# The sink logit as a column of the score tile, in a step of windowed attention

## The chip, the cores and the metric

The kernel runs on one core of one Trainium2 chip. The metric is the device time of one execution in microseconds (us). The engines are TensorE (PE; its weight loads are shown apart as PEld), VectorE (DVE), ScalarE (ACT), GpSimd (POOL) and SyncE (SP), which issues most of the DMAs.

## The reference

One inference step of a two-layer network over 128 context and 1024 latent tokens. Each layer has a token mixer of three groups (windowed softmax attention, gated linear attention, a recurrent unit) and an MLP. The change concerns the softmax of the attention group: 8 heads of 64 in 2 key groups, blocks of 128 queries, and per head one learned sink logit that takes part in the maximum and in the denominator and has no value row.

```python
def softmax_with_sink(scores, sink):
    m = sink
    for s in scores:
        m = jnp.maximum(m, jnp.max(s, axis=-1, keepdims=True))
    es = [jnp.exp(s - m) for s in scores]
    denom = jnp.exp(sink - m)
    for e in es:
        denom = denom + jnp.sum(e, axis=-1, keepdims=True)
    inv = 1.0 / denom
    return [e * inv for e in es]
```

A latent block sees its own, the previous and the next block of keys (masked to a distance of 128) and all 128 context keys in one softmax; a context block sees context keys alone.

## The kernel before

All arithmetic is fp32, with every matmul operand split into a high and a low part, so that a product is three matmuls (`dense`, lines 151 to 159), or two where one side is not split. `Net.layer` runs mixer, attention, output projection and MLP of one layer after the other.

`attention` works through 18 steps in each layer, one for a query block i and a key group g with four heads each, and a 19th turn that only finishes the last. In turn n, `scores` makes the scores of step n: per head two matmuls of up to 512 columns (L1061) into a PSUM bank, and one DVE instruction (L1063) that scales them, adds the mask, writes them to a tile P in SBUF and leaves the maximum, started from the sink logit, in a column of m. `soft` turns two heads at a time into probabilities: it negates m (L1072), adds the sink (L1073), takes the exponential of that (L1074, ACT), takes the exponential of P with bias m and the row sum (L1076, ACT), adds the two sums (L1077), inverts (L1078), and multiplies P by the inverse on POOL (L1080). The first half of `soft` is called inside `scores` after the second head, the second half later, between the pieces of `values`, which in the same turn works on the step before: it transposes P block by block on TensorE (L1089), splits it into ph (ACT, L1092) and pl (DVE, L1093) and multiplies with the values (L1098). A tile P has eight buffers, so two steps of four.

Between these pieces `attention` calls `fill` (in `layer`), which puts other TensorE work there: half an output tile of the output projection at a time (`out_half`, L1204 to L1211: two passes of two inputs with three matmuls each, 384 columns), and pieces of the modulation matrix (L249). Every fourth turn has one more half tile. The weights of the output projection are loaded and split by `load_w` (L117 to L119); in most of these stretches the subtraction L119 of 128x1024 runs on POOL.

TensorE's instructions stand in the order of the code. On the other engines a scheduler sets the order when the program is built, by its own estimate of when operands are there; every engine works through its list in order, so an instruction that waits holds all behind it. PSUM has five banks of `pg` for scores, transposes and values, two of `pd` for the output projection.

Of the kernel before, what the change touches and what calls it, by code (L numbers as in the profile page):

```python
# [48 lines left out]
class Net:  # L49
# [951 lines left out]
    def attention(self, l, fill):  # L1001
# [7 lines left out]
        nc.sync.dma_start(sink, I["attn_sink"][l:l + 1].to_broadcast([128, 8]))  # L1009
        for i in range(2, 4):  # L1010
            self.pre_q(0, i)
        def load_v():
# [34 lines left out]
        def scores(i, g, Q):  # L1047
            c0 = 128 * (i % 3)
            kpos, npos, vb, mk = geom(i)
            W = 128 * npos  # L1050
            m = ap.tile([128, 4], F32, tag="m", name="m", bufs=3)
            dn = ap.tile([128, 4], F32, tag="dn", name="dn", bufs=3)
            es = ap.tile([128, 4], F32, tag="es", name="es", bufs=3)
            Ps = []
            sc = (Ps, m, dn, es, W)
            for j in range(4):
# [3 lines left out]
                for ki, K in enumerate((KH[g], KL[g])):  # L1060
                    nc.tensor.matmul(ps[:, :W], q, K[:, kpos:kpos + npos].rearrange("p b c -> p (b c)"), start=ki == 0, stop=ki == 1)  # L1061
                P = ap.tile([128, 512], F32, tag="P", name="P", bufs=8)
                nc.vector.tensor_tensor_reduce(P[:, :W], ps[:, :W], mask[:, mk], scale=0.125, scalar=sink[:, h:h + 1],  # L1063
                                               op0=ALU.add, op1=ALU.max, accum_out=m[:, j:j + 1])
                Ps.append(P)
                if j == 1:
                    soft(g, 0, *sc)
            return sc

        def soft(g, part, Ps, m, dn, es, W):  # L1070
            js = slice(2 * part, 2 * part + 2)
            nc.vector.tensor_scalar(m[:, js], m[:, js], -1.0, None, ALU.mult)  # L1072
            nc.vector.tensor_tensor(es[:, js], sink[:, 4 * g + 2 * part:4 * g + 2 * part + 2], m[:, js], ALU.add)  # L1073
            nc.scalar.activation(es[:, js], es[:, js], AF.Exp)  # L1074
            for j in range(2 * part, 2 * part + 2):
                nc.scalar.activation(Ps[j][:, :W], Ps[j][:, :W], AF.Exp, bias=m[:, j:j + 1], accum_out=dn[:, j:j + 1])  # L1076
            nc.vector.tensor_tensor(dn[:, js], dn[:, js], es[:, js], ALU.add)  # L1077
            nc.vector.reciprocal(dn[:, js], dn[:, js])  # L1078
            for j in range(2 * part, 2 * part + 2):
                nc.gpsimd.tensor_scalar(Ps[j][:, :W], Ps[j][:, :W], dn[:, j:j + 1], 1.0, ALU.mult, ALU.mult)  # L1080

# [42 lines left out]
        for n in range(19):  # L1124
            if n < 18:
# [14 lines left out]
                sc = scores(i, g, Q)  # L1140
                if n == 1:
                    k1()
            if n:
                fill(n, 1)
                for k, _ in enumerate(values(*pend)):
                    if n < 18 and k == 1:
                        soft(g, 1, *sc)
                    fill(n, 2 + k)
            else:
                soft(g, 1, *sc)  # L1150
                load_v()
                k1 = self.load_k(l, 1, ap)
            pend = (i, g, sc[0])
# [373 lines left out]
```

## Time and profile before

| | us |
|---|---|
| runs (3), median (lowest to highest) | 2958.36 (2957.66 to 2959.3) |
| span of the profiled execution | 2958.0 |
| PE busy | 2765.4 |
| DVE busy | 1591.8 |
| ACT busy | 1069.0 |
| POOL busy | 796.3 |

The profile is of one execution; its span goes from the first to the last instruction and holds nearly all of its time. Matmuls overlap in the pipeline, so PE's busy time counts more than the time in which it delivers columns. Attention is the stretch from about 446 to 638 us in layer 0 and from 1892 to 2083 us in layer 1.

### The profile page before, as it was taken

Reading aid. Unit: us, or ns where it says so; the run is one execution under the profiler, and the core shown is the slowest. Engines: PE = TensorE matmul, PEld = TensorE weight load, DVE = VectorE, ACT = ScalarE, POOL = GpSimd, SP = SyncE. Lnnn points to the kernel's source line nnn. Section 1 sums busy time; section 2 is a strip of 40 time slices with the busy share of each in tenths; the row PEclk is TensorE's granted clock in tenths of the full one; section 3 lists DMA queues with packets and bytes.
Section 4 is the critical chain, followed back from the end, with each engine's and each line's share of the span. In section 5 each row is a group of like instructions: output and inputs, shape, how many; then the busy total and the mean of one; then the engine's idle time right before and its main releaser. Section 6 shows DMA issues by size and latency. Waiting matters only on the chain.

```text
span 2958.0 us, 41898 instructions
## 1 busy us (share of the span) xinstructions
PE 2765.4 (93%) x16067; PEld 2628.4 (89%) x16067; DVE 1591.8 (54%) x3032; ACT 1069.0 (36%) x2029; POOL 796.3 (27%) x807
## 2 busy tenths in 40 slices
PE   5897988989999999999987989899899999999998
PEld 3786987789999999999987879777899999999998
DVE  7668578896332332233478577888932332233235
ACT  4424446764122112211354326477622112211223
POOL 5323445652011001100133334466411001100112
PEclk7998999999999999999999999999999999999999
DMA  7535347411321111111333643662211111111113
GB/s 258 133 109 148 117 136 244 140 61 53 98 94 43 43 43 43 43 43 43 98 109 90 174 132 103 200 197 75 72 43 43 43 43 43 43 43 40 40 44 129
DMA packets 279304, 273.66 MB, mean 93 GB/s; under 512 B 30032, under 2 KB 259008, under 8 KB 279104
## 3 DMA queue, kind: packets, MB, share of 16 engines
q1 hardware_dynamic: 278888, 270.92, 29.7%
q8 instruction: 127, 2.08, 0.3%
q14 instruction: 73, 0.60, 0.1%
q10 hardware_dynamic: 216, 0.06, 0.0%
HBM read 227.02 MB, written 43.91 MB: 92 GB/s over the span
## 4 chain that ended last, share of the span: by engine, by line
PE 71%; DVE 16%; issue 4%; ACT 4%; POOL 3%; DMA 2%; SPq 0%; DVEq 0%; POOLq 0%; ACTq 0%
PE pg L155 18%; PE pg L156 18%; PE pg L157 18%; PE pd L155 2%; PE pd L156 2%; PE pd L157 2%; DVE B L672 2%; PE pg L1098 2%; PE pg L1061 1%; PE pe L249 1%; PE pd L1204 1%; DVE P L1063 1%; PE pd L1205 1%; PE pd L1206 1%; DVE wl L119 1%
## 5 line engine op out<-in xcount | busy, mean ns | idle before, releaser
L118 ACT CAST wh<-wr 128x1024 fp32r<-128x1024 f32 x228 | 238.9, 1048 | 931.1 <-PE pg L156 826.0
L156 PE MATMUL pg<-hl,wh 128*128 128x384 f32 x1584 | 538.3, 340 | 2.7 <-DVE hl L345 1.5
L155 PE MATMUL pg<-hh,wh 128*128 128x384 f32 x1584 | 538.8, 340 | 1.8 <-ACT hh L344 1.8
L157 PE MATMUL pg<-hh,wl 128*128 128x384 f32 x1584 | 537.4, 339 | 0.0
L1247 POOL TENSOR_TENSOR te<-te 128x384 f32<-128x384 f32 x192 | 166.7, 868 | 1331.5 <-ACT uh L1246 1331.3
L155 PE MATMUL pg<-uh,wh 128*128 128x384 f32 x1536 | 515.0, 335 | 0.6 <-ACT wh L118 0.6
L157 PE MATMUL pg<-uh,wl 128*128 128x384 f32 x1536 | 514.0, 335 | 1.7 <-DVE wl L119 1.7
L156 PE MATMUL pg<-ul,wh 128*128 128x384 f32 x1536 | 513.9, 335 | 0.0
L1269 DVE SCALAR_TENSOR_TENSOR x<-pg,mod,x 128x384 f32<-128x384 f32 (+2 forms) x512 | 254.1, 515 | 396.5 <-PE pg L157 396.3
L1248 DVE TENSOR_TENSOR ul<-te,uh 128x384 fp32r<-128x384 f32 x192 | 107.1, 558 | 452.6 <-POOL te L1247 452.6
L119 DVE TENSOR_TENSOR wl<-wr,wh 128x1024 fp32r<-128x1024 f32 x196 | 244.9, 1249 | 191.3 <-ACT wh L118 191.2
L155 PE MATMUL pd<-hh,wh 128*128 128x384 f32 x816 | 295.3, 362 | 24.8 <-DVE te L480 9.5
L155 PEld LDWEIGHTS pg<-hh,wh 128*128 128x128 f32 x1584 | 299.6, 189 | 5.4 <-issue 3.4
L156 PEld LDWEIGHTS pg<-hl,wh 128*128 128x128 f32 x1584 | 299.5, 189 | 5.1 <-DVE hl L351 2.5
L157 PEld LDWEIGHTS pg<-hh,wl 128*128 128x128 f32 x1584 | 299.3, 189 | 0.0
L155 PEld LDWEIGHTS pg<-uh,wh 128*128 128x128 f32 x1536 | 288.8, 188 | 4.3 <-issue 1.7
L157 PEld LDWEIGHTS pg<-uh,wl 128*128 128x128 f32 x1536 | 288.9, 188 | 2.1 <-DVE wl L119 2.0
L156 PEld LDWEIGHTS pg<-ul,wh 128*128 128x128 f32 x1536 | 288.8, 188 | 0.0
L156 PE MATMUL pd<-hl,wh 128*128 128x384 f32 x816 | 284.6, 349 | 3.4 <-DVE hl L385 3.4
L157 PE MATMUL pd<-hh,wl 128*128 128x384 f32 x816 | 284.0, 348 | 0.0
L1245 ACT ACTIVATE te<-pg 128x384 f32<-128x384 f32 x192 | 94.0, 489 | 358.9 <-PE pg L157 358.9
L155 PEld LDWEIGHTS pd<-hh,wh 128*128 128x128 f32 x816 | 161.2, 198 | 34.5 <-DVE te L480 10.8
(275 smaller groups left out, 4457.2 us busy)
## 6 DMA issues: line engine op xcount, KB each, us to landing
wr<-in_w_mlp_dram SPq DMA_DIRECT2D x144, 512.0 KB
wm<-in_w_mod_dram SPq DMA_DIRECT2D x96, 512.0 KB
wr<-in_w_out_dram SPq DMA_DIRECT2D x48, 512.0 KB
wr<-in_w_in_dram SPq DMA_DIRECT2D x36, 512.0 KB
xd<-x SPq DMA_DIRECT2D x48, 192.0 KB
x<-xd SPq DMA_DIRECT2D x48, 192.0 KB
raw<-mixd SPq DMA_DIRECT2D x40, 192.0 KB
B<-gkd SPq DMA_DIRECT2D x16, 288.0 KB
```

Source lines behind the costliest of these rows:

```text
L118: nc.scalar.copy(hi[:, :m], raw[:, :m])
L119: lo_eng.tensor_tensor(lo[:, :m], raw[:, :m], f32(hi[:, :m]), ALU.subtract)
L155: mm(out, wh[i], xs[i][0], start=i == 0, stop=False)
L156: mm(out, wh[i], xs[i][1], start=False, stop=False)
L157: mm(out, wl[i], xs[i][0], start=False, stop=i == n - 1)
L249: nc.tensor.matmul(p[32 * g:32 * g + 32, :], self.cs[:, kt, :], ws[g // 2][:, 512 * (g % 2):512 * (g % 2) + 512], start=kt == 0, stop=kt = ...
L672: nc.vector.scalar_tensor_tensor(out, Sc[r, c], dec[r, c:c + 1], dc[r, c], ALU.mult, ALU.add)
L1098: nc.tensor.matmul(po, VS[g][:, vb[b]], K, start=b == 0 and ki == 0, stop=b == npos - 1 and ki == 1)
L1245: nc.scalar.activation(r, p[:, :TB], AF.Relu)
L1247: nc.gpsimd.tensor_tensor(r, r, r, ALU.mult)
L1248: nc.vector.tensor_tensor(blk(ul, tb), r, f32(blk(uh, tb)), ALU.subtract)
L1269: nc.vector.scalar_tensor_tensor(xa, p[:, a:b], self.M[l]["g2"][:, dt, s:s + 1], xa, ALU.mult, ALU.add)
```

## The change

The sink is negated once per layer (nsink). Scores are written negated (scale -0.125), with a running minimum that starts from the negated sink, so that m holds the negated maximum without a further instruction. P becomes a tile of 4 rows of 513 elements for all four heads, held in two fixed buffers by the parity of the step; scores are written right-aligned, up to column 511, and column 512 holds the negated sink, copied by POOL (L1058 of the changed kernel). One exponential with scale -1 covers the scores and the sink column, and its row sum is the whole denominator. The lines L1072, L1073, L1074 and L1077 are gone. The line numbers of the changed kernel are 4 to 5 higher at the scores and 1 higher at the exponential; L1078, L1080 and those behind stay.

```diff
@@ -1007,8 +1007,12 @@
         nc.sync.dma_start(mask, C["c_amask"])
         sink = ap.tile([128, 8], F32, name="sink")
         nc.sync.dma_start(sink, I["attn_sink"][l:l + 1].to_broadcast([128, 8]))
+        nsink = ap.tile([128, 8], F32, name="nsink")
+        nc.vector.tensor_scalar(nsink, sink, -1.0, None, ALU.mult)
+        PT = [ap.tile([128, 4, 513], F32, name=f"P{k}") for k in range(2)]
         for i in range(2, 4):
             self.pre_q(0, i)
+
         def load_v():
             vraw = self.kp.tile([128, 10, 128], F32, tag="raw", name="vraw")
             nc.sync.dma_start(vraw[:, 0:9], self.vd.rearrange("j p c -> p j c"))
@@ -1044,40 +1048,36 @@
                 return 8, 3, [9, 7, 8], slice(0, 384)
             return KPOS[n - 1], 4, ([n, 9, n + 1, n + 2] if n % 2 == 0 else [n, n + 1, 9, n + 2]), slice(128, 640)
 
-        def scores(i, g, Q):
+        def scores(n, i, g, Q):
             c0 = 128 * (i % 3)
             kpos, npos, vb, mk = geom(i)
             W = 128 * npos
+            P = PT[n % 2]
             m = ap.tile([128, 4], F32, tag="m", name="m", bufs=3)
             dn = ap.tile([128, 4], F32, tag="dn", name="dn", bufs=3)
-            es = ap.tile([128, 4], F32, tag="es", name="es", bufs=3)
-            Ps = []
-            sc = (Ps, m, dn, es, W)
+            nc.gpsimd.tensor_copy(P[:, :, 512], nsink[:, 4 * g:4 * g + 4])
+            Ps = [P[:, j, 512 - W:512] for j in range(4)]
+            sc = (P, Ps, m, dn, W)
             for j in range(4):
                 h = 4 * g + j
                 ps = self.pg()
                 q = Q[h][:, c0:c0 + 128]
                 for ki, K in enumerate((KH[g], KL[g])):
                     nc.tensor.matmul(ps[:, :W], q, K[:, kpos:kpos + npos].rearrange("p b c -> p (b c)"), start=ki == 0, stop=ki == 1)
-                P = ap.tile([128, 512], F32, tag="P", name="P", bufs=8)
-                nc.vector.tensor_tensor_reduce(P[:, :W], ps[:, :W], mask[:, mk], scale=0.125, scalar=sink[:, h:h + 1],
-                                               op0=ALU.add, op1=ALU.max, accum_out=m[:, j:j + 1])
-                Ps.append(P)
+                nc.vector.tensor_tensor_reduce(Ps[j], ps[:, :W], mask[:, mk], scale=-0.125, scalar=nsink[:, h:h + 1],
+                                               op0=ALU.add, op1=ALU.min, accum_out=m[:, j:j + 1])
                 if j == 1:
-                    soft(g, 0, *sc)
+                    soft(0, *sc)
             return sc
 
-        def soft(g, part, Ps, m, dn, es, W):
+        def soft(part, P, Ps, m, dn, W):
             js = slice(2 * part, 2 * part + 2)
-            nc.vector.tensor_scalar(m[:, js], m[:, js], -1.0, None, ALU.mult)
-            nc.vector.tensor_tensor(es[:, js], sink[:, 4 * g + 2 * part:4 * g + 2 * part + 2], m[:, js], ALU.add)
-            nc.scalar.activation(es[:, js], es[:, js], AF.Exp)
             for j in range(2 * part, 2 * part + 2):
-                nc.scalar.activation(Ps[j][:, :W], Ps[j][:, :W], AF.Exp, bias=m[:, j:j + 1], accum_out=dn[:, j:j + 1])
-            nc.vector.tensor_tensor(dn[:, js], dn[:, js], es[:, js], ALU.add)
+                e = P[:, j, 512 - W:513]
+                nc.scalar.activation(e, e, AF.Exp, bias=m[:, j:j + 1], scale=-1.0, accum_out=dn[:, j:j + 1])
             nc.vector.reciprocal(dn[:, js], dn[:, js])
             for j in range(2 * part, 2 * part + 2):
-                nc.gpsimd.tensor_scalar(Ps[j][:, :W], Ps[j][:, :W], dn[:, j:j + 1], 1.0, ALU.mult, ALU.mult)
+                nc.gpsimd.tensor_scalar(Ps[j], Ps[j], dn[:, j:j + 1], 1.0, ALU.mult, ALU.mult)
 
         def values(i, g, Ps):
             kpos, npos, vb, mk = geom(i)
@@ -1137,20 +1137,20 @@
                     Q = {}
                     for j in range(4):
                         load_q(n // 6, j)
-                sc = scores(i, g, Q)
+                sc = scores(n, i, g, Q)
                 if n == 1:
                     k1()
             if n:
                 fill(n, 1)
                 for k, _ in enumerate(values(*pend)):
                     if n < 18 and k == 1:
-                        soft(g, 1, *sc)
+                        soft(1, *sc)
                     fill(n, 2 + k)
             else:
-                soft(g, 1, *sc)
+                soft(1, *sc)
                 load_v()
                 k1 = self.load_k(l, 1, ap)
-            pend = (i, g, sc[0])
+            pend = (i, g, sc[1])
         self.close(ag)
 
     def out_open(self, l):
```

The scheduler's order around it, in step 8 of layer 0 (query block 3, second key group). On DVE before, from the second score on (P and m carry numbers of their instances, es and dn too; pd is the output projection's bank):

```order
L1063 ISA P_4971,m_4960<-pg_4968,amask_4062,sink_4064 128x512 [waits PE_49,Pool_49]
L1063 ISA m_4960 128x1
L1063 ISA P_4985,m_4960<-pg_4982,amask_4062,sink_4064 128x512 [waits PE_49,Pool_49]
L1063 ISA m_4960 128x1
L1072 TENSOR_SCALAR m_4960<-m_4960 128x2 [waits DVE_49]
L1063 ISA P_4990,m_4960<-pg_4987,amask_4062,sink_4064 128x512 [waits PE_49,Pool_49]
L1063 ISA m_4960 128x1
L1073 TENSOR_TENSOR es_4962<-sink_4064,m_4960 128x2 [waits DVE_49]
L1211 SCALAR_TENSOR_TENSOR x5_3774<-pd_4911,mod0_1_2864,x5_3774 128x384 [waits DMAHW7_49,PE_49]
L1072 TENSOR_SCALAR m_4960<-m_4960 128x2 [waits DVE_49]
L1073 TENSOR_TENSOR es_4962<-sink_4064,m_4960 128x2 [waits DVE_49]
L1077 TENSOR_TENSOR dn_4961<-dn_4961,es_4962 128x2 [waits Activation_49]
```

On DVE now, the same place:

```order
L1067 ISA P1_4069,m_4880<-pg_4887,amask_4062,nsink_4066 128x512 [waits PE_49,Pool_49]
L1067 ISA m_4880 128x1
L1067 ISA P1_4069,m_4880<-pg_4896,amask_4062,nsink_4066 128x512 [waits PE_49,Pool_49]
L1067 ISA m_4880 128x1
L1067 ISA P1_4069,m_4880<-pg_4900,amask_4062,nsink_4066 128x512 [waits PE_49,Pool_49]
L1067 ISA m_4880 128x1
L1211 SCALAR_TENSOR_TENSOR x5_3774<-pd_4831,mod0_1_2864,x5_3774 128x384 [waits PE_49]
L1078 RECIPROCAL dn_4881<-dn_4881 128x2 [waits Activation_49]
L1093 TENSOR_TENSOR pl_4926<-pg_4920,ph_4925 128x512 [waits DVE_49,Activation_49]
L1093 TENSOR_TENSOR pl_4935<-pg_4929,ph_4934 128x512 [waits DVE_49,Activation_49]
L1078 RECIPROCAL dn_4881<-dn_4881 128x2 [waits Activation_49]
```

The scores follow one another, and the output projection's L1211 and the reciprocal come right behind; L1072, L1073 and L1077 have gone from between. The reciprocal itself now waits for ACT.

On ACT before, in the same step (ph is the split of the transposed probabilities of the step before):

```order
L1076 ACTIVATE P_4966,dn_4961<-P_4966,m_4960 128x512 [waits DVE_49,Pool_49]
L1076 ACTIVATE P_4971,dn_4961<-P_4971,m_4960 128x512 [waits Pool_49]
L1074 ACTIVATE es_4962<-es_4962 128x2 [waits DVE_49]
L1092 CAST ph_5013<-pg_5008 128x512 [waits PE_49,Activation_49]
L1092 CAST ph_5022<-pg_5017 128x512 [waits PE_49,Activation_49]
L1074 ACTIVATE es_4962<-es_4962 128x2 [waits DVE_49]
L1076 ACTIVATE P_4985,dn_4961<-P_4985,m_4960 128x512 [waits Pool_49]
L1092 CAST ph_5038<-pg_5033 128x512 [waits PE_49,Activation_49]
L1092 CAST ph_5049<-pg_5044 128x512 [waits PE_49,Activation_49]
L1076 ACTIVATE P_4990,dn_4961<-P_4990,m_4960 128x512 [waits Pool_49]
```

On ACT now (L118 is the cast of an output weight; x2 is two rows alike):

```order
L1077 ACTIVATE P1_4069,dn_4881<-P1_4069,m_4880 128x513 [waits DVE_49,Pool_49]
L118 CAST wh_5047<-wr_5046 128x1024 [waits DMAHW1_49,PE_49]
L1077 ACTIVATE P1_4069,dn_4881<-P1_4069,m_4880 128x513 [waits DVE_49]
L1092 CAST ph_4925<-pg_4920 128x512 [waits PE_49,Activation_49]
L1092 CAST ph_4934<-pg_4929 128x512 [waits PE_49,Activation_49]
L1077 ACTIVATE P1_4069,dn_4881<-P1_4069,m_4880 128x513 [waits DVE_49] x2
L1092 CAST ph_4950<-pg_4945 128x512 [waits PE_49,Activation_49]
L1092 CAST ph_4961<-pg_4956 128x512 [waits PE_49,Activation_49]
```

The exponentials of the second half now stand together ahead of the third cast of ph; the fourth exponential stood behind the fourth cast. A weight cast stands between the first two exponentials, where it stood ahead of them.

On POOL before, from the weight subtraction on:

```order
L119 TENSOR_TENSOR wl_5148<-wr_5146,wh_5147 128x1024 [waits DMAHW1_49,PE_49,Activation_49]
L1080 TENSOR_SCALAR P_4966<-P_4966,dn_4961 128x512 [waits DVE_49,Activation_49]
L1080 TENSOR_SCALAR P_4971<-P_4971,dn_4961 128x512 [waits Activation_49]
L1080 TENSOR_SCALAR P_4985<-P_4985,dn_4961 128x512 [waits DVE_49,Activation_49]
L1080 TENSOR_SCALAR P_4990<-P_4990,dn_4961 128x512 [waits Activation_49]
```

On POOL now:

```order
L119 TENSOR_TENSOR wl_5048<-wr_5046,wh_5047 128x1024 [waits DMAHW1_49,PE_49,Activation_49]
L1080 TENSOR_SCALAR P1_4069<-P1_4069,dn_4881 128x512 [waits DVE_49]
L1080 TENSOR_SCALAR P1_4069<-P1_4069,dn_4881 128x512 [waits Activation_49]
L1058 COPY P1_4069<-nsink_4066 128x4 [waits Activation_49,Pool_49]
L1080 TENSOR_SCALAR P1_4069<-P1_4069,dn_4881 128x512 [waits DVE_49]
L1080 TENSOR_SCALAR P1_4069<-P1_4069,dn_4881 128x512
```

The copy of the sink into the buffer that step 10 will use stands between the normalisations of the two halves, and waits for the exponentials of this step.

## Rows read from the trace of the kernel before

**Rows 1.** Windows: us, busy PE, PEld, DVE, ACT, POOL (instructions), PEclk, DMA share, GB/s.

```profile
446.00:638.00 192.00, 176.65 (x966) 146.14 (x964) 161.81 (x455) 136.73 (x330) 117.80 (x125) 0.97 0.49 155
1892.00:2083.00 191.00, 174.34 (x968) 144.31 (x968) 163.04 (x455) 137.30 (x331) 117.46 (x124) 0.99 0.48 150
```

**Rows 2.** The chain of waits by line, in these two stretches, shares of each.

```profile
by line: PE pg L1098 13.2%; PE pg L1061 9.5%; issue 8.7%; DVE P L1063 7.8%; PE pd L1206 6.1%; PE pd L1205 6.0%; PE pd L1204 6.0%; DVE es L1073 5.6%; DVE pl L1093 5.6%; PE pg L1089 5.0%; PE pe L249 4.0%; DVE x L1211 3.7%; DVE m L1072 2.3%; A
...
by line: PE pg L1098 12.7%; PE pg L1061 9.8%; issue 8.1%; DVE P L1063 7.2%; DVE pl L1093 5.9%; DVE es L1073 5.6%; PE pg L1089 5.5%; PE pd L1204 5.2%; PE pd L1205 5.1%; PE pd L1206 5.0%; PE pe L249 3.6%; DVE x L1211 3.6%; ACT P L1076 3.1%; D
```

**Rows 3.** Groups, VectorE, 446 to 638: busy us, mean ns, idle before.

```profile
L1073 DVE TENSOR_TENSOR es<-sink,m 128x2 f32<-128x2 f32 x36 | 17.2, 479 | 0.2
L1072 DVE TENSOR_SCALAR m<-m 128x2 f32<-128x2 f32 x36 | 9.0, 250 | 0.1
L1077 DVE TENSOR_TENSOR dn<-dn,es 128x2 f32<-128x2 f32 x36 | 7.3, 203 | 2.2 <-ACT es L1074 1.3 <-ACT P L1076 0.6
```

**Rows 4.** Single lines of VectorE: ns minimum, median, maximum; first and last start.

```profile
L1073 DVE TENSOR_TENSOR es<-sink,m x72: 145/160/2130, 452.7 to 2072.4; 128x2 f32<-128x2 f32 x72
...
L1093 DVE TENSOR_TENSOR pl<-pg,ph x124: 669/680/694, 462.1 to 2081.1; 128x512 fp32r<-128x512 f32 x124
...
L1078 DVE RECIPROCAL dn<-dn x72: 147/166/168, 455.7 to 2075.3; 128x2 f32<-128x2 f32 x72
```

**Rows 5.** The timeline around 520: start us, us, instruction, idle time before it.

```profile
520.05 0.72 ACT L1076 ACTIVATE P<-P,m 128x512 f32<-128x512 f32 x1
520.23 2.38 POOL L119 TENSOR_TENSOR wl<-wr,wh 128x1024 fp32r<-128x1024 f32 x1 [2.83 <-ACT wh L118]
520.51 2.12 DVE L1073 TENSOR_TENSOR es<-sink,m 128x2 f32<-128x2 f32 x1
522.66 0.20 ACT L1074 ACTIVATE es<-es 128x2 f32<-128x2 f32 x1 [1.09 <-DVE es L1073]
```

**Rows 6.** Pieces of the chain, 500 to 560: start us, us, what.

```profile
516.25 0.95 PE pg L1061 x4
520.59 2.04 DVE es L1073
527.71 1.85 PE pg L1061 x8
538.69 1.86 PE pg L1061 x8
548.64 0.94 PE pg L1061 x4
559.85 0.23 PE pg L1061
```

**Rows 7.** The chain by line from 528 to 548.

```profile
by line: PE pg L1089 19.8%; PE pg L1061 17.5%; PE pg L1098 17.2%; PE pd L1206 12.3%; PE pd L1205 12.3%; PE pd L1204 12.2%; PE pe L249 10.0%
```

**Rows 8.** Who waited for L1080, and who for L1072: us, times.

```profile
  PEld pg L1089: 8.7, 17
...
  ACT P L1076: 19.8, 18
```

**Rows 9.** Groups and one line of GpSimd, columns as in rows 3 and 4.

```profile
L1080 POOL TENSOR_SCALAR P<-P,dn 128x384 f32<-128x384 f32 x32 | 19.5, 624 | 17.5 <-DVE es L1073 4.3 <-DVE dn L1078 3.8 <-ACT es L1074 3.3
...
L1080 POOL TENSOR_SCALAR P<-P,dn 128x128 f32<-128x128 f32 x16 | 8.0, 513 | 21.0 <-DVE dn L1078 10.3 <-ACT vs L1019 9.8 <-PE pe L249 0.4
...
L311 POOL TENSOR_TENSOR rs<-ms,nhalf x15: 850/864/1152, 30.3 to 2950.1; 128x3 f32<-128x3 f32 x15
```

**Rows 10.** Groups of VectorE's line 815, whole span.

```profile
L815 DVE SCALAR_TENSOR_TENSOR B<-B,vt 128x1023 f32<-128x1023 f32 x8 | 10.2, 1272 | 0.0
L815 DVE SCALAR_TENSOR_TENSOR B<-B,vt 128x127 f32<-128x127 f32 x8 | 2.7, 339 | 0.0
```

**Rows 11.** Groups of TensorE's weight loads, 446 to 638.

```profile
L1089 PEld LDWEIGHTS pg<-ident,P 128*128 128x128 f32 x248 | 29.6, 141 | 9.9 <-POOL P L1080 4.5 <-DVE m L1072 1.7 <-DVE dn L1078 0.8
L1061 PEld LDWEIGHTS pg<-kh,qs 128*128 128x128 f32 x72 | 13.6, 189 | 2.1
```

## The prediction

> **What bounds the kernel now.** I read the windows of the two attention stretches first, because all edited lines run there. In 192 us of layer 0 and 191 us of layer 1, TensorE is busy 177 and 174 us, VectorE (DVE) 162 and 163, ScalarE (ACT) 137 in each, GpSimd (POOL) 118 and 117; the granted clock is 0.97 and 0.99 and the DMA engines are half used [rows 1]. Two engines are near full, so busy time alone doesn't say which sets the end; the chain of waits does. Within both stretches it changes between TensorE's lines and DVE's. Of the lines that the change removes, L1073 holds 5.6% of both stretches and L1072 2.3% of the first (the second row ends before L1072 appears) [rows 2].
>
> Second, the groups of instructions and the lines themselves. L1073 adds two columns to two columns, yet takes 479 ns in the mean, L1072 250 and L1077 203 [rows 3]. L1073's median is 160 ns and its maximum 2130. L1093, 512 columns with one operand in PSUM, stays between 669 and 694, and the reciprocal L1078, on the same two columns, between 147 and 168 [rows 4]. One case shows what happens: POOL starts a weight subtraction of 2.38 us at 520.23; L1073 starts at 520.51 and ends at 522.63, 0.02 us after it; ACT's small exponential then starts at 522.66 [rows 5]. So the tiny DVE instructions are held by POOL, and DVE's queue behind them with them.
>
> Third, steps in the chain. From 516.25 to 527.71 (11.46 us) the chain passes through that held L1073 for 2.04 us. From 527.71 to 538.69 and on to 548.64 (10.98 and 9.95 us) [rows 6] the chain is TensorE alone [rows 7]. The code gives the first of these two one more half output tile. The 9.95 us step holds the same matmuls as the one from 516.25, so that is the floor.
>
> **The change part by part.** In each half of a step's softmax the negation of m (L1072), the add with the sink (L1073), its exponential (L1074) and the add to the sum (L1077) go; the large exponential takes one more column instead. That is 36 instructions of each line per layer, three lines on DVE and one on ACT. Nothing else on DVE gets longer: the scores' instruction keeps its form, with another sign, a minimum and no negation behind it. One negation of eight columns per layer is new on DVE, which I cost at nothing: it runs before the first score, beside the casts of q. An exponential of 513 columns instead of 512 I cost at nothing too.
>
> First term, the chain: 7.9% of 192 us is 15.2 us; for layer 1, 10.7 us of L1073 and the same 4.4 of L1072. Together 30.3 us [rows 2]. L1077 is on the chain only in pieces under 0.2 us, and I leave it out.
>
> What is late next: the step at 516.25 can't fall below 9.95, so of its 2.04 us at most 1.5 come back. The one from 548.64 to 559.85 is 11.21 us, 1.26 above the floor [rows 6]. ACT then takes part of it: in the new order both exponentials of the second half stand ahead of the third cast of ph, where one of them stood behind the fourth. I let 55% of 30.3 through: -16.7 us. The bounds are 0 and, if every step gave up the same share as 11.46 to 9.95, 13% of 383 us, 50 us.
>
> The weighing of busy time: the excess of L1073 over its median, 36 times 319 ns, is 11.5 us a layer, nearly all of its 10.7 us on the chain. If it were a wait that any DVE instruction there would suffer, the next ones would show it too; the reciprocal's maximum of 168 ns speaks against that [rows 3, 4]. The Trainium skill ("SBUF — State Buffer", section "Who interferes with whom") says that a VectorE instruction with two SBUF inputs and a GpSimd one that reads SBUF exclude each other for a whole instruction, while one with at most one SBUF input outside the two-port modes is not held. By that rule the excess goes for good and the term above stands; without it, 11.5 of the 15.1 us a layer would move to the reciprocal, the first term would be 55% of 7.3 us, 4 us, and the sum 2955 us.
>
> Second term, ACT: an exponential now waits for its own head's minimum, where L1072 used to wait for two heads and stand behind the third. ACT waited 19.8 us for L1072 in 18 waits [rows 8]. Most of that is the chain's again; I count a fifth on top, -4 us (bounds 0 and -10). ACT also loses 72 instructions L1074 of about 0.2 us [rows 5], which helps where it is the late one; that is in the 55%.
>
> Third term, POOL: 36 copies of 128x4, each two steps ahead of the exponential that reads it, so that no exponential waits for one. But the copy stands between the normalisations of the first and the second half, and waits for the last exponential. Its cost isn't in the trace: POOL's multiply by a scalar takes 624 ns at 384 columns and 513 at 128, which is 0.46 at none, and the three-column L311 864 [rows 9]. I take 0.46, by the nearest form. The reciprocal of about 0.17 us [rows 4] runs beside it; 0.29 are left. TensorE's transposes waited for POOL's normalisation 17 times [rows 8]: +4.9 us. The bounds are 0, where they hide behind the wait for the last exponential, and, at 0.86 in all 36 steps, +25.
>
> Fourth, the rows: the rows of P for heads 1 to 3 now start 4, 8 and 12 bytes off, since a row has 513 elements. DVE's line L815 works on such rows: 1272 ns at 1023 columns and 339 at 127 are 1.04 ns a column beyond a fixed part [rows 10], where L1093's 512 columns take 1.33 ns each with the fixed part [rows 4]; so DVE is not slower there. For ACT, POOL and TensorE no row shows it. Lower bound nil; upper bound: transposes' weight loads of 141 ns becoming the 189 of the score's [rows 11], 48 ns on three quarters of twice 248, +18 us, and ACT's exponentials longer by the same third. I take nil, as on DVE.
>
> Scheduling also moves two things at no cost: x loads of the next third of the tokens stand behind the second head group's keys on SP's queue; they are used only several steps later. The subtraction L992 in step 2 moves ahead of its fourth score, which delays that head and brings the keys for step 3 earlier.
>
> Sum: -16.7 - 4 + 4.9 = -15.8 us. The profiled span is 2958.0 us, 0.4 below the median of the runs, so the change is set against 2958.4: 2942.6, and I say 2942 us. Behind attention TensorE bounds the stages and their weights are fetched as buffers free, so the time gained stays gained.
>
> **The rivals.** (a) DVE was the only late link: steps fall to TensorE's floor. For it: two neighbouring steps already run there [rows 7]. Against: ACT is busy 137 of 192 us and its order got worse. 30 to 50 us less, 2908 to 2928.
>
> (b) ACT takes DVE's place: exponentials 3 and 4 ahead of the third cast cost TensorE 0.2 to 0.3 us in each of 36 steps, 8 to 11 us, and leave 5 to 8 of the 16. For it: ACT's P is 3.1% of the second chain [rows 2]. Result 2950 to 2953.
>
> (c) Slower: the unaligned rows cost every engine that reads them what a score's weight load costs over a transpose's, a third. TensorE's 18 us have no cover in steps that it already bounds [rows 7]. ACT's 108 exponentials of heads 1 to 3, 0.72 us each [rows 5], gain 0.24 us, 26 us, half of it on the path since ACT is the next late engine: 13. Against the 16 us gained that is 15 more, 2973. It decides from about 43 ns a weight load (16 us over 372 loads), sooner if ACT's part counts. For it: all three engines read those rows, and nothing in the trace shows one on them. Against: DVE's L815 [rows 10].
>
> (d) No change: TensorE's queue was the real limit and the chain's DVE pieces lay beside slack. 2958. For it: copies at L311's price, +25, would leave about this. Against: the held step of 11.46 beside 9.95 [rows 6].
>
> **How the numbers follow.** Forecast 0.58, (a) 0.11, (b) 0.19, (c) 0.07, (d) 0.05. What a measurement can tell from no change is 0.2%, 6 us. Faster: the forecast, (a) and two thirds of (b), 0.82. Same: the rest of (b), where ACT takes more, and most of (d), 0.10. Slower: (c) and a little of (d), 0.08. The range leaves out most of (a) at one end and (c) at the other: 2920 to 2957; the forecast's own is 2931 to 2952.
>
> **What would show it.** In the new profile the attention stretches are 7 to 10 us shorter each, DVE's busy time in them falls from 162 to near 130 us, no small DVE instruction exceeds 0.2 us, and the chain has more TensorE and ACT. Copies on POOL take 0.3 to 0.6 us. Forecast and mechanism are wrong if DVE's busy time falls as said and the stretches don't shorten (then (b) or (d)), if transposes wait for POOL in most steps (copies), or if the exponentials, normalisations or transposes themselves got longer (c).

## The result, and the profile after

The changed kernel takes 2930.02 us (median of 4 runs, 2926.49 to 2932.37) beside 2958.83 for the kernel before (median of 4, 2957.66 to 2962.26): ratio 0.9894, 95% interval 0.9879 to 0.9908, some 29 to 31 us less. The forecast was 2942; the time lies inside its range and just below the forecast's own one. The direction and the place were right, the size, 15.8 us, was about half of what came.

The windows of the two attention stretches, with the columns of [rows 1] and cut near the same places (the second of [rows 1] begins 2.5 us ahead of its first score, the other three 3.7 to 3.8; all four end within 0.6 us of the last matmul with the values):

```profile
442.00:620.60 178.60, 170.52 (x973) 144.36 (x974) 138.47 (x352) 134.04 (x295) 124.49 (x144) 0.99 0.54 170
1871.90:2049.50 177.60, 170.55 (x969) 144.66 (x969) 139.01 (x351) 133.97 (x294) 124.81 (x144) 0.98 0.52 165
```

Each window is 13.4 us shorter (192 to 178.6, 191 to 177.6). With the same edges in all four, from the first score's weight load to the end of the last matmul with the values, it is 13.9 and 14.1 us, 28.0 together, against 28.8 between the medians. DVE works 23 to 24 us less in each; the three lines were 33.5 busy [rows 3], but a held instruction lies partly beside its neighbours on the same engine: without these lines DVE was busy for 139.6 and 138.9 us before. TensorE is now busy for 95% of the first stretch, where it was 92%.

The weight loads of the first score and of the first score of the eighteenth and last step give a measure free of the edges: first the kernel before, then the changed one, layer 0 (start, us).

```profile
449.81 0.19 PEld L1061 LDWEIGHTS pg<-kh,qs 128*128 128x128 f32 x1
...
623.25 0.19 PEld L1061 LDWEIGHTS pg<-kh,qs 128*128 128x128 f32 x1
```

```profile
445.68 0.19 PEld L1066 LDWEIGHTS pg<-kh,qs 128*128 128x128 f32 x1
...
605.85 0.19 PEld L1066 LDWEIGHTS pg<-kh,qs 128*128 128x128 f32 x1
```

Seventeen steps last 173.4 us before and 160.2 after. The first score comes 4.1 us earlier, but ahead of it nothing has changed save one negation of eight columns on DVE (0.17 us) and the first copy on POOL; in the profiles of the experiments below it starts between 445.07 and 451.66, so this isn't taken as the change's.

The chain of waits by line over the second stretch's steps from 1926 on (it answers the second row of [rows 2]), and the scores' pieces in it (start, us):

```profile
by line: PE pg L1098 19.7%; PE pg L1066 15.0%; PE pg L1089 12.2%; PE pd L1205 9.6%; PE pd L1204 9.6%; PE pd L1206 9.4%; PE pe L249 5.7%; issue 3.8%; DVE pl L1093 3.4%; DVE P L1067 2.3%; ACT P L1077 2.1%; ACT ph L1092 2.0%; ACT qs L1036 1.8%
...
1928.40 1.82 PE pg L1066 x8
1937.03 1.87 PE pg L1066 x8
1946.77 1.84 PE pg L1066 x8
1957.58 1.86 PE pg L1066 x8
1967.68 1.84 PE pg L1066 x8
```

TensorE's lines hold 81% of this chain, all eight score matmuls of a step are in the chain, where the held steps of [rows 6] had four, and the steps are 8.63, 9.74, 10.81 and 10.10 us long. They answer, one layer on, to the steps of [rows 6]: 9.74 to the 11.46 from 516.25, and 10.81 and 10.10 to the 10.98 and 9.95 that were TensorE's alone before and had next to nothing to give.

The groups after, first VectorE and GpSimd, then ScalarE and the weight loads (busy us, mean ns, idle before), and the reciprocal's minimum, median and maximum:

```profile
L1093 DVE TENSOR_TENSOR pl<-pg,ph 128x512 fp32r<-128x512 f32 x62 | 40.6, 685 | 12.1 <-ACT ph L1092 11.9
L1078 DVE RECIPROCAL dn<-dn 128x2 f32<-128x2 f32 x36 | 5.8, 161 | 5.2 <-ACT P L1077 4.6
...
L1080 POOL TENSOR_SCALAR P<-P,dn 128x512 f32<-128x512 f32 x48 | 33.0, 701 | 8.9 <-DVE dn L1078 6.0 <-PE pd L1206 2.4
L1080 POOL TENSOR_SCALAR P<-P,dn 128x384 f32<-128x384 f32 x16 | 11.2, 708 | 4.3 <-DVE dn L1078 4.1 <-PE pg L1089 0.2
L1058 POOL COPY P<-nsink 128x4 f32<-128x4 f32 x18 | 3.7, 207 | 4.2 <-ACT P L1077 3.4 <-DVE nsink L1011 0.8
...
L1077 ACT ACTIVATE P<-P,m 128x513 f32<-128x513 f32 x48 | 34.7, 727 | 7.6 <-DVE m L1067 7.3
L1092 ACT CAST ph<-pg 128x512 fp32r<-128x512 f32 x62 | 34.1, 589 | 1.9 <-PE pg L1089 1.4
...
L1089 PEld LDWEIGHTS pg<-ident,P 128*128 128x128 f32 x248 | 29.6, 140 | 7.6 <-DVE pl L1093 2.5 <-POOL P L1080 1.6 <-issue 0.8
L1098 PEld LDWEIGHTS pg<-ph,vs 128*128 128x128 f32 x62 | 12.0, 193 | 7.3 <-ACT ph L1092 3.2 <-ACT wh L118 1.7 <-ACT mh L1180 0.8
...
L1078 DVE RECIPROCAL dn<-dn x72: 144/166/168, 450.6 to 2042.1; 128x2 f32<-128x2 f32 x72
```

The reciprocal is the one small DVE instruction of the softmax that is left, and it isn't held (maximum 168 ns, as before): the hold has not moved to it. The transposes' weight loads wait 1.6 us for POOL where it was 4.5 [rows 11] and take 140 ns as before. There are 18 copies in a layer, one per step for all four heads; each takes 0.21 us.

### The profile page after: what moved, and what is told of

Same layout as the page of the kernel before. It is cut to its first block, busy times and chain, and to the rows that moved or that the text cites. A ratio compares the mean times of both kernels' runs of the same rounds, so it can differ in the third digit from the quotient of the medians.

```text
span 2924.7 us, 41719 instructions
## 1 busy us (share of the span) xinstructions
PE 2749.6 (94%) x16067; PEld 2621.1 (90%) x16067; DVE 1540.2 (53%) x2818; ACT 1062.2 (36%) x1957; POOL 807.7 (28%) x843
## 3 DMA queue, kind: packets, MB, share of 16 engines
q1 hardware_dynamic: 278888, 270.92, 30.3%
## 4 chain that ended last, share of the span: by engine, by line
PE 63%; DVE 7%; ACT 2%; issue 2%; POOL 1%; DMA 1%; SPq 0%; POOLq 0%; DVEq 0%; ACTq 0%
PE pg L156 18%; PE pg L155 18%; PE pg L157 18%; DVE B L672 1%; PE pd L155 1%; PE pg L1098 1%; PE pd L156 1%; PE pd L157 1%; PE pg L1066 1%; DVE tn L343 1%; PE pe L249 1%; PE pd L1204 1%; PE pd L1205 1%; PE pd L1206 1%; PE pg L1089 1%
## 5 line engine op out<-in xcount | busy, mean ns | idle before, releaser
L118 ACT CAST wh<-wr 128x1024 fp32r<-128x1024 f32 x228 | 239.0, 1048 | 918.2 <-PE pg L156 826.1
L119 DVE TENSOR_TENSOR wl<-wr,wh 128x1024 fp32r<-128x1024 f32 x196 | 244.9, 1250 | 191.1 <-ACT wh L118 190.9
```

The lines of the kernel that those rows point to most:

```text
L118: nc.scalar.copy(hi[:, :m], raw[:, :m])
L119: lo_eng.tensor_tensor(lo[:, :m], raw[:, :m], f32(hi[:, :m]), ALU.subtract)
```

## The experiments

The theory after this look: POOL holds the small DVE instructions of the softmax, and what stood behind them paid. The rivals: that fewer instructions or hops explain it, that the exponentials' shorter wait does, or ACT's lighter load. Six runs put one thing back into the changed kernel, three take one part or two out of the kernel before, one changes what POOL does there, and two test the prediction's terms for rows and copies. The table gathers all: ratio to the kernel before, run beside it, with its interval; the time between the two weight loads shown above, in layer 0 and layer 1; the last twelve of these seventeen steps alone, since the first five hold pieces at a lower granted clock that differ from run to run (e2 has 0.66 in the mean from 1895 to 1905 us, the changed kernel 1.00), while in the last twelve it is 1.00 in every run but e1 in layer 0 and e8 (0.99); and mean ns of the small instructions in layer 0. The changed kernel's own ratio comes from the first measurement; e9, e11 and e12, which cost nothing, lie at 0.990 in another.

| kernel | ratio (95%) | 17 steps, us | last 12 | small DVE instructions |
|---|---|---|---|---|
| before | 1 | 173.4, 173.1 | 127.3, 127.3 | L1072 250, L1073 479, L1077 203 |
| changed | 0.9894 (0.9879-0.9908) | 160.2, 159.7 | 117.4, 117.2 | none |
| e1 changed, unread add | 0.9934 (0.9919-0.9949) | 165.7, 162.9 | 123.2, 119.9 | 455 |
| e2 changed, unread reciprocal | 0.9912 (0.9895-0.9929) | 161.4, 164.6 | 116.9, 118.0 | 156 |
| e3 before, no negation | 0.9979 (0.9967-0.9991) | 170.6, 169.4 | 125.3, 124.7 | 338, 474 |
| e4 before, no sink add | 1.0009 (0.9997-1.0022) | 172.1, 172.9 | 127.6, 127.4 | 457, 214 |
| e5 before, neither | 0.9975 (0.9964-0.9986) | 168.3, 170.6 | 124.3, 126.4 | 376 |
| e6 changed, held, exps wait | 0.9969 (0.9956-0.9981) | 167.2, 168.5 | 123.1, 123.0 | 434 |
| e7 changed, not held, exps wait | 0.9939 (0.9927-0.9952) | 164.0, 163.0 | 120.6, 121.4 | 158 |
| e8 before, L119 on DVE | 0.9991 (0.9981-1.0001) | 172.8, 172.1 | 126.6, 126.6 | 311, 262, 171 |
| e9 changed, small exps back | 0.9901 (0.9884-0.9919) | 160.2, 158.0 | 117.4, 116.9 | none |
| e10 changed, held at reciprocal | 0.9925 (0.9908-0.9943) | 164.4, 162.1 | 120.9, 119.4 | 494 |
| e11 changed, 516-column rows | 0.9900 (0.9882-0.9918) | 157.7, 158.2 | 117.0, 117.9 | none |
| e12 changed, copies gone | 0.9899 (0.9882-0.9917) | 159.8, 157.7 | 116.7, 117.4 | none |

**Is it the hold, or the instruction?** e1 and e2 put one small instruction per half back in the same places; nothing reads its result. The other engines' order is nearly the same in both.

```diff
+ nc.vector.tensor_tensor(es[:, js], nsink[:, 4*g+2*part:4*g+2*part+2], m[:, js], ALU.add)   # e1
+ nc.vector.reciprocal(es[:, js], m[:, js])                                                   # e2
```

> The changed kernel, with one instruction added per half of a softmax: an add of two columns of nsink and two of m on DVE, whose result nothing reads; it stands where L1073 stood. Theory (POOL holds a DVE instruction that reads two SBUF operands, and DVE's queue waits behind it): its mean is 350 to 550 ns, with a maximum above 1.5 us, and the time rises by 8 to 19 us over the changed kernel, 2938 to 2949. Rival (only the number of DVE instructions and the hops between engines counted): its mean is about 160 ns, as is L1073's median, and 72 of them cost at most 3 us, 2930 to 2933.

> The changed kernel, with a reciprocal of two columns of m added in the same places, one SBUF operand, result unread. Theory: it isn't held, mean 150 to 170 ns, and the time stays within 3 us of the changed kernel, 2928 to 2933. Rival (any DVE instruction there is delayed, or counts the same): the same time as the run with two operands.

The added line's minimum, median and maximum in e1 and one case there (start, us), and then the same line of e2:

```profile
L1076 DVE TENSOR_TENSOR es<-nsink,m x72: 133/156/1869, 452.6 to 2058.3; 128x2 f32<-128x2 f32 x72
...
578.64 2.38 POOL L119 TENSOR_TENSOR wl<-wr,wh 128x1024 fp32r<-128x1024 f32 x1 [1.24 <-ACT wh L118]
579.16 1.87 DVE L1076 TENSOR_TENSOR es<-nsink,m 128x2 f32<-128x2 f32 x1
```

```profile
L1076 DVE RECIPROCAL es<-m x72: 140/156/167, 452.3 to 2056.0; 128x2 f32<-128x2 f32 x72
```

The add is held as L1073 was (mean 455 ns, as expected): it starts 0.52 us after POOL's subtraction and ends 0.01 us behind it. The reciprocal is never held. e1's ratio is 0.0040 above the changed kernel's, about 12 us, as expected; e2's 0.0018, 5 us, more than the 3 expected, though its interval overlaps the changed kernel's. In the last twelve steps e2 costs nothing (116.9 and 118.0 beside 117.4 and 117.2), e1 2.7 us in layer 1. In layer 0 one step of e1, the one with the case shown, is 13.37 us long, and this is the clock as well: TensorE waited 2.43 us for DVE's work behind the held add, and from 584 to 587.7 us its granted clock was 0.61 in the mean, for the most part the lower of its two levels (1.2 of 2.4 GHz), with 0.52 us for a matmul of 384 columns that took 0.33 before. So a held instruction costs even where nobody needs its result, because DVE's queue stands behind it. What a free one costs lies between nothing, by the last twelve steps, and 5 us, by the ratio; the intervals of e1 and e2 overlap, and it is the holds and the last twelve steps that tell the two apart.

**One part alone.** e3 takes the negation out of the kernel before, e4 the sink's add.

```diff
- op0=ALU.add, op1=ALU.max ... scale=0.125 ... nc.vector.tensor_scalar(m, m, -1.0)     # e3
+ op0=ALU.add, op1=ALU.min ... scale=-0.125, exponentials with scale=-1.0
- nc.vector.tensor_tensor(es[:, js], sink[...], m[:, js], ALU.add); exp(es[:, js])      # e4
+ nc.scalar.activation(es[:, j:j+1], sink[:, h:h+1], AF.Exp, bias=m[:, j:j+1])   # per head
```

> The kernel before, with one part of the change alone: scores evicted negated with a running minimum and exponentials with scale -1, so that L1072 goes; L1073, the small exponential and L1077 stay. Theory (L1072 held 2.3% of the stretches' chain, L1073 5.6%): 9 us of the chain go, and the time falls by 5 to 10 us to 2949 to 2954; the add's mean stays at 400 to 550 ns. Rival (the gain came from the exponentials that wait for their own head alone): most of the 29 us comes with this part, 2930 to 2938.

> The kernel before, with L1073 alone taken from DVE: ACT makes the sink's exponential head by head from the sink and m as the bias (36 more small instructions on ACT per layer, about 0.2 us each). Theory: L1073's 10.7 us a layer of the chain go, and the time falls by 10 to 20 us to 2938 to 2948, although ACT does more. Rival (ACT is the late engine, the gain came from its 72 small exponentials): slower than before by 2 to 10 us.

e3 came as expected in time (-6 us), but the sink's add fell to 338 ns, below the 400 to 550 expected. e4 brought no gain: +2.7 us, which lies in its rival's 2 to 10, though its interval holds no change as well; e9 below puts that rival, ACT as the late engine, to the test in the changed kernel. The groups say why. First e3's, then e4's, with e4's longest case:

```profile
L1078 DVE TENSOR_TENSOR dn<-dn,es 128x2 f32<-128x2 f32 x36 | 17.1, 474 | 6.3 <-ACT es L1075 4.5 <-ACT P L1077 1.6
L1074 DVE TENSOR_TENSOR es<-sink,m 128x2 f32<-128x2 f32 x36 | 12.2, 338 | 0.0
```

```profile
L1072 DVE TENSOR_SCALAR m<-m 128x2 f32<-128x2 f32 x36 | 16.5, 457 | 0.1
L1077 DVE TENSOR_TENSOR dn<-dn,es 128x2 f32<-128x2 f32 x36 | 7.7, 214 | 7.8 <-ACT P L1076 7.4
...
479.07 2.39 POOL L119 TENSOR_TENSOR wl<-wr,wh 128x1024 fp32r<-128x1024 f32 x1
479.31 2.17 DVE L1072 TENSOR_SCALAR m<-m 128x2 f32<-128x2 f32 x1
481.52 0.48 ACT L1074 ACTIVATE es<-sink,m 128x1 f32<-128x1 f32 x2 [2.29 <-DVE m L1072]
```

The hold moves. Without the negation the denominator's add goes from 203 to 474 ns; without the sink's add the negation goes from 250 to 457 [rows 3]. POOL works on; whichever small instruction comes next meets it. The negation has one SBUF operand and is held for 2.17 us all the same. The Trainium skill ("SBUF — State Buffer", section "Who interferes with whom") counts `tensor_scalar` among the instructions that can enter a two-port mode and then contend with GpSimd; this trace agrees.

**Two parts at once.** e5 is e3 and e4 together; only the denominator's add is left.

> The kernel before with both other parts at once: scores evicted negated with a minimum (no L1072), and the sink's exponential made on ACT head by head (no L1073, 36 more small ACT instructions per layer). Of the three small DVE instructions only the add dn+es is left. Theory, mended after the first runs (POOL's hold is taken by whichever of the small instructions comes next, so taking one away moves it; what counts is what waits behind it): the add's mean is 0.4 to 0.55 us, but no exponential waits behind it any more, and the time falls by 10 to 20 us against before. Rival (the parts add up independently, -6 us of the negation and +2 of the add): -2 to -6 us.

-7 us: short of the 10 to 20 that the mended theory gave, and just past the rival's 2 to 6 (the interval, -4 to -11 us, reaches into both). Its add takes 376 ns, a little under the 400 expected, and no exponential waits behind it. But ACT pays for the sink's exponentials head by head:

```profile
L1075 ACT ACTIVATE es<-sink,m 128x1 f32<-128x1 f32 x72 | 19.6, 294 | 9.0 <-DVE m L1065 8.5
```

That is 19.6 us a stretch where the kernel before had 7.3 (36 of 202 ns). e10 below has a held add in the same place without that work and is 0.0050 faster, so these small exponentials are the likely rest; it wasn't run apart, and e10 has the changed kernel's tile P as well. So e4 and e5 measure their replacement too.

**Where it is held.** e6 puts a held instruction ahead of the exponentials, e7 two that aren't held, e10 one ahead of the reciprocal.

```diff
+ nc.vector.tensor_tensor(m[:, js], m[:, js], m[:, js], ALU.max)        # e6, ahead of the exponentials
+ for _ in range(2): nc.vector.reciprocal(m[:, js], m[:, js])           # e7, the same place
+ nc.vector.tensor_tensor(dn[:, js], dn[:, js], dn[:, js], ALU.max)     # e10, ahead of the reciprocal
```

> The changed kernel with one DVE instruction per half put back where L1072 was: m becomes the larger of m and m, two SBUF operands, the same value; the exponentials wait for it. Theory: it is held like L1073 (mean 350 to 550 ns), both exponentials of a half wait for it, and 15 to 25 us of the 31 come back, twice what the same held instruction cost where nothing waited for it (12). Rival (the wait behind it is nothing, only DVE's time counts): 8 to 14 us over the changed kernel. Second rival (count of instructions alone): at most 3.

> As the last, but with two reciprocals in a row of m's two columns (one SBUF operand each, m as it was up to rounding) in the place of the one instruction with two operands. Theory: none is held, mean 150 to 170 ns each, the exponentials wait 0.3 us more and for both heads: 3 to 10 us over the changed kernel, and less than half of what the held one costs. Rival (what counts is the wait of the exponentials for both heads' minimum, not the hold): the same as the held one within 3 us.

> The changed kernel with a held instruction in the third place, where L1077 was: dn becomes the larger of dn and dn (two SBUF operands, same value) between the exponentials and the reciprocal, so that reciprocal, normalisation and the next step's transposes wait for it. Theory: its mean is 350 to 500 ns; with nothing on ACT behind it, it costs 6 to 14 us over the changed kernel, more than or as much as the one whose result is unread (4 us in each stretch), less than the one before the exponentials (8 in each). Rival (the wait in this place is hidden, since the transposes come later anyway): at most 4 us.

Single lines, minimum, median and maximum, in e6, e7 and e10:

```profile
L1075 DVE TENSOR_TENSOR m<-m x72: 132/156/1977, 447.6 to 2058.9; 128x2 f32<-128x2 f32 x72
```

```profile
L1076 DVE RECIPROCAL m<-m x144: 132/159/168, 451.7 to 2056.8; 128x2 f32<-128x2 f32 x144
```

```profile
L1078 DVE TENSOR_TENSOR dn<-dn x72: 134/182/2185, 450.5 to 2056.0; 128x2 f32<-128x2 f32 x72
```

In seventeen steps, mean of the two layers over the changed kernel's 159.9: e6 +7.9, e7 +3.6, e10 +3.3, and e1 +4.4. By the ratios e6 gives 22 us back, e7 13, e10 9. So e6's place is the dearest, as expected. e7's 13 us are above the 3 to 10 expected, and more than half of e6's; neither its theory nor its rival (within 3 us of e6) came true. e7 shares with e6 the wait for both heads' minimum and the hop through DVE, and this may be a part of e6's price that is not the hold. How much is not shown: e7's two reciprocals take 0.32 us together, not far from the held instruction's mean of 0.43, and in e6 and e7 the scheduler put many instructions of ACT and DVE in another order, while in e1, e2 and e10 it kept the changed kernel's almost wholly. e10's mean of 494 ns and its 9 us are in the range expected; that it costs at least as much as e1 is not shown (9 us against 12, with intervals that overlap).

**Who holds.** e8 moves the weights' subtraction from POOL to DVE in the kernel before.

```diff
- 4, nc.vector if (tb, half) in ((0, 1), (2, 0)) else nc.gpsimd)
+ 4, nc.vector)
```

> The kernel before, with the weights' low parts of attention (L119) subtracted on DVE in all half tiles, never on POOL, where one takes 2.4 us: 16 of them per layer leave POOL, and 16 of about 1.1 us come to DVE. Theory (POOL's instruction holds the small ones for as long as it runs, so the long ones hold most): the three means of L1073, L1072 and L1077, 932 ns together, fall below 700, L1073's maximum of 2.1 us goes below 1.2; DVE pays about 18 us a layer of work for it, so the time is -5 to +15 us against before. Rival (POOL doesn't hold them; it is DVE's own pipeline or something else): the sum of the three stays above 850 ns.

```profile
L1072 DVE TENSOR_SCALAR m<-m 128x2 f32<-128x2 f32 x36 | 11.2, 311 | 0.1
L1073 DVE TENSOR_TENSOR es<-sink,m 128x2 f32<-128x2 f32 x36 | 9.4, 262 | 0.2
...
L1073 DVE TENSOR_TENSOR es<-sink,m x72: 145/158/950, 449.2 to 2077.6; 128x2 f32<-128x2 f32 x72
```

L1073's maximum falls from 2130 to 950 ns, as long as POOL's remaining instructions (L1034 and L1181 take 1.0 us), and the three means from 932 to 744 in sum: between theory's 700 and the rival's 850, nearer the theory. In time next to nothing is left of it, within what was expected, as DVE now does these subtractions; one step of each layer, at 12.4 us where it was 11.4, also had a granted clock of 0.86.

e8 could take only a part, since L119 is not the only holder. One case of the kernel before shows the rest (start, us): in the same subtraction L1034 the reciprocal goes through, and the add behind it is held to the end.

```profile
554.47 1.00 POOL L1034 TENSOR_TENSOR qs<-te,qs 64x384 fp32r<-64x384 f32 x1
...
554.57 0.17 DVE L1078 RECIPROCAL dn<-dn 128x2 f32<-128x2 f32 x1
554.65 0.84 DVE L1073 TENSOR_TENSOR es<-sink,m 128x2 f32<-128x2 f32 x1
```

In the whole trace 52 of the 216 instances of L1072, L1073 and L1077 take over 300 ns, and each of the 52 ends 4 to 29 ns after an instruction of POOL: 12 after L119, 40 after others of 0.7 to 1.0 us. The same holds for every long one of e1, e3 to e6, e8 and e10 (0 to 31 ns after). Of e7's 144 added reciprocals 59 start with over 0.2 us of a POOL instruction still to run, and none of them takes over 168 ns. So it is POOL that holds, and a reciprocal is let through.

**ACT, rows and copies.** e9 puts ACT's small exponential back into the changed kernel, e11 makes the rows of P 516 columns apart, e12 copies the sink's column in the first two steps alone.

```diff
+ nc.scalar.activation(es[:, js], nsink[:, 4*g+2*part:4*g+2*part+2], AF.Exp)      # e9
- PT = [ap.tile([128, 4, 513], F32, ...    # e11
+ PT = [ap.tile([128, 4, 516], F32, ...
+ if n < 2:                                # e12, ahead of the copy
```

> The changed kernel with ACT's small exponential put back alone: one of two columns of nsink per half, result unread, waiting for nothing. It takes about 0.2 us, 36 of them 7 us of ACT in a stretch. Theory (TensorE bounds the steps of the changed kernel, ACT has room there): at most 3 us over the changed kernel in the stretches together, ratio to before 0.989 to 0.991. Rival (ACT is the late engine and its small exponentials were a good part of the gain): 7 to 14 us over the changed kernel, 0.992 to 0.994.

> The changed kernel with rows of P at a pitch of 516 columns instead of 513, so that the rows of all four heads start on 16 bytes; the order of the instructions is the same. Theory (unaligned rows cost nothing): 0 to 2 us from the changed kernel, ratio to before 0.988 to 0.991, weight loads of the transposes 140 ns and exponentials 0.73 us as they were; POOL's multiply at 384 columns (708 ns after, 624 before) may go back. Rival (the rows cost up to a third on some engine): 5 to 15 us faster than the changed kernel.

> The changed kernel with POOL's copy of the sink's column in the first two steps of each layer alone (this leaves the refilling of the column out of the other sixteen), 32 of 36 copies gone. Theory (a copy of 0.21 us, hidden beside the reciprocal and in front of it): 0 to 3 us faster than the changed kernel, 0.988 to 0.990. Rival (the copy waits for the last exponential and delays the normalisations behind it, as the prediction's +4.9 us): 4 to 8 us faster, 0.986 to 0.988.

One row of e9, two of e11, one of e12 (the multiply, L1080 of the changed kernel):

```profile
L1076 ACT ACTIVATE es<-nsink 128x2 f32<-128x2 f32 x36 | 4.8, 196 | 2.2 <-DVE nsink L1011 2.2
```

```profile
L1080 POOL TENSOR_SCALAR P<-P,dn 128x384 f32<-128x384 f32 x16 | 11.1, 708 | 4.3 <-DVE dn L1078 4.1 <-PE pg L1089 0.2
...
L1089 PEld LDWEIGHTS pg<-ident,P 128*128 128x128 f32 x248 | 29.6, 141 | 5.8 <-DVE pl L1093 2.5 <-issue 0.8 <-POOL P L1080 0.2
```

```profile
L1081 POOL TENSOR_SCALAR P<-P,dn 128x384 f32<-128x384 f32 x16 | 11.1, 708 | 4.7 <-DVE dn L1079 4.4 <-PE pg L1090 0.2
```

All three lie at 0.990, on the changed kernel within what these runs can tell (the intervals are 0.0035 wide, 10 us). The last twelve steps are the closer measure: 116.7 to 117.9 beside 117.4 and 117.2. By them ACT has room for the small exponentials (which here wait for nothing, where L1074 waited for L1073), and neither the rows nor the copies cost anything. No variant beats the changed kernel.

## Why the prediction was right, and where it was off

**What is held, and why (right).** A small instruction with two SBUF operands put back is held again (e1), a reciprocal isn't (e2, e7), the longest holds go when POOL's long instruction goes (e8), and every long one ends with an instruction of POOL. The prediction's reading of [rows 3 to 5] stands. The other reading, by which the wait would have passed to the reciprocal (sum 2955), fell: the reciprocal's maximum is still 168 ns.

**The first term (mis-sized; the step that failed).** The prediction let 55% of the chain's 30.3 us through, 16.7. The two stretches of seventeen steps lost 13.3 and 13.4, 26.7 together, 88%; this holds the second term's 4 as well. Of it 20.0 came in the last twelve steps, at a granted clock of 1.00 before and after. The reason given for the other 45%, that both exponentials of the second half stand ahead of the third cast of ph, cost nothing that shows. TensorE's wait for that cast fell from 6.9 us (the kernel before, its windows and columns as in [rows 11]) to 3.2 in the row of L1098 above:

```profile
L1098 PEld LDWEIGHTS pg<-ph,vs 128*128 128x128 f32 x62 | 12.1, 195 | 11.2 <-ACT ph L1092 6.9 <-ACT P L1076 1.7 <-ACT wh L118 0.8
```

And 36 small exponentials more per layer on ACT are free (e9). ACT was not the next late engine; TensorE was, at its floor. That floor was read nearly right: the step of 11.46 us fell to 9.77, so 1.7 came back, where 1.5 were allowed. But one share was then laid on all steps. By the same weight loads, eight of the last twelve steps of layer 0 lost 0.7 to 1.7 us each and the other four 0 to 0.2, so what each step lay above its own floor, added up, was the better sum. An estimate shows it: seven of these steps hold TensorE's work of the 9.95 us step of [rows 6], three as it is and four without the eight pieces of L249, which take 1.00 us. By these two floors they lay 8.3 us above them before, and they lost 7.0.

**L1077 (left out, wrongly).** It was on the chain only in pieces, but put back alone in its place a held instruction costs 3.3 us a stretch (e10). As part of the three it mattered because the hold moves: it took 474 ns with the negation gone (e3) and 376 with the other two gone (e5). No run with one or two of the three gone gained more than 7 us; that the whole gain needs all three to go is likely but not shown apart, since e4 and e5 carry more work on ACT.

**The second term.** That the exponentials no longer wait for both heads is worth at most 3.6 us a stretch by e7's seventeen steps (which have two more DVE instructions and another order as well), 7 in both, and at most 13 by its ratio, beside 4 estimated and 10 as its bound. No run shows it apart.

**The third term (wrong size).** A copy takes 207 ns, not 460, and with 16 of 18 per layer gone the last twelve steps change by -0.7 and +0.2 us (e12). The +4.9 was nil, its lower bound.

**The rows (right).** e11 has the same time and the same 141 ns. POOL's multiply at 384 columns did go from 624 to 708 ns, but stays at 708 with rows on 16 bytes, so that isn't the rows. It is the hold the other way round. In layer 0 twelve of the sixteen take 580 to 597 ns, and four 747 to 1474, where the kernel before had one of 1140. Each of these starts while DVE is in an instruction with two SBUF operands, as here (start, us):

```profile
457.44 1.21 DVE L119 TENSOR_TENSOR wl<-wr,wh 128x1024 fp32r<-128x1024 f32 x1
...
457.62 1.47 POOL L1080 TENSOR_SCALAR P<-P,dn 128x384 f32<-128x384 f32 x1 [0.92 <-DVE dn L1078]
```

**The rivals.** (b) fell with the time itself, and e9 shows room on ACT. (a) was right in kind: the later steps are at TensorE's floor or near it (81% of the chain above); but its 30 to 50 us took more than the steps had, and 29 to 31 came. (c) and (d) fell. The marks set out before: the stretches 13 to 14 us shorter, not 7 to 10; DVE busy 138, not near 130, which counted as the three lines' own what they shared with neighbours; copies 0.21 us, below 0.3; no small instruction above 0.2 us, as said.

**What stays open.** The parts put back one at a time cost 4.4, 7.9 and 3.3 us a stretch, 15.6 in sum, the parts taken out one at a time give 3.3 and 0.8: they don't add, and the moving hold explains the direction, not each number. How much of e5's time is its small exponentials, and how much of e6's is the wait for both heads, was not run apart. About 4 us of the profiled span's difference of 33.3 lies ahead of attention and comes from the run.

## What to carry to other kernels

When one engine holds small instructions of another, count what can be held, not only what the chain names: taking away one of three moves the wait to the next, taking away all three ends it. An instruction that is held ends just behind the one that holds it, so the trace names the holder before any run is made. Before discounting a gain for the next late engine, look whether that engine really waits or only looks busy; here an engine busy for 75% had room, and the limit was the neighbouring step that was already at TensorE's floor. A test that replaces an instruction measures the replacement too.

## What the runs showed of the hardware

A negation of two columns (one SBUF operand) is held by POOL up to 2175 ns (e4), and a reciprocal of two columns never takes over 168. In the cases looked at the one that started first held the other: POOL's multiply of 384 columns, mostly 580 to 597 ns in the changed kernel, took 1474 where it started 0.18 us into a DVE subtraction of 1.21. An exponential of one column with a column of bias takes 294 ns, one of two columns without 196 to 204. A copy of four columns on POOL takes 207 ns in the mean, where its multiply came to 568 at 128 columns. POOL's multiply at 384 columns had means from 585 to 714 ns over these kernels; in the kernel before and the changed one the difference is how many of them DVE holds.
